# Moving the 2 KB tiles of a two-block network to one run of SBUF addresses

## Chip, core and metric

The kernel runs on one core of one Trainium2 chip. The metric is device time in microseconds, as the median of a few executions. Times inside the kernel come from one execution that the hardware profiler recorded.

## What is computed

The input is 512 tokens of width 1024, in float32. It goes through two blocks of two layers each. In outline:

```python
def first_block(x, ...):          # twice
    p = rmsnorm(x) @ w_in         # latents for attention, and a gated branch
    y_attn = attention(...)       # 8 heads, low-rank q and kv, rotary part
    u = silu(layernorm(dwconv31(a * sigmoid(gt))))
    x = x + concat(y_attn, u) @ w_o
    z = dwconv3(rmsnorm(x) @ w_up)        # 2 * 2816 columns
    x = x + (silu(zg) * zv) @ w_down
def second_block(x, ...):         # layer 0: ssd mixer, layer 1: hgrn2 mixer
    h = layer_norm(ALPHA * x + mixer(x))
    h = layer_norm(ALPHA * h + relu(h @ w1)**2 @ w2)    # 4096 columns
    x = h + sigmoid(h @ w_gate) * (p @ w_proj)
```

All weights are float32 and are read from HBM once, 232.5 MB in all.

## The kernel before

Activations lie transposed: channels on the 128 partitions, the 512 tokens along the free axis. One such tile of float32 takes 2048 bytes in each partition. Nearly everything that is computed with lives in tiles of this size, class `s`; 86 places for them exist (`SLOTS`, line 617). Smaller classes are `r` (3 places of 4096 bytes, where raw weights land), `u` (4 of 2168 bytes, with margins for convolutions), `t` (512 bytes), `n` (up to 128 bytes), and one tile each for the vectors `V` and the constants `C`.

A product in nearly full precision is made of three single-pass float32r matmuls (`mm3`, line 717; `dense`, line 722). An activation and a weight are each split into a rounded part "hi" and the rest "lo" (`pair`, `split_from`, lines 636 and 727; `weights`, line 689), and the three matmuls are hi by hi, lo by hi and hi by lo. Each streams 512 columns (256 where a stage works on half of the tokens, `HALVES`, line 623) past 128x128 weights. The moving operand is a whole `s` tile or a half of it, and the weights are a 512-byte slice of an `s` tile. So both operands of these matmuls start at the address of an `s` tile plus a multiple of 512 bytes. The weights of matmul k+1 are loaded while matmul k streams.

The order of all work is laid down beforehand. Operations are first recorded, then a planner (`schedule`, line 464) gives each one an engine, a place in the order and, for each new tile, a place of its class that is free by then. `issue` (line 589) then writes the instructions out; all of them pass through line 599, which is why the profile shows that line everywhere and the reader has to go by tile names. The planner knows nothing of addresses.

Addresses are given while the instructions are written: `alloc` in `build` asks the pool for the tile the first time that a place is used, and the pool hands out the next free bytes, rounded up to 32. So before the change the classes are mixed in the order of first use. The first byte of the pool is 16512 in each partition. The places of class `s` come to lie as follows:

| places | first byte | last start | start modulo 512 | start modulo 256 |
|---|---|---|---|---|
| s0 to s22 | 30656 | 80320 | 448 | 192 |
| s23 to s44 | 84544 | 136256 | 64 | 64 |
| s45, s46 | 138336 | 140384 | 96 | 96 |
| s47 to s52 | 142464 | 152704 | 128 | 128 |
| s53 | 154816 | 154816 | 192 | 192 |
| s54 to s85 | 156992 | 220480 | 320 | 64 |

Among them lie `V`, `C`, `r`, `u`, some of `t` and `n`; the rest of `t` and `n` end at byte 226784. The `r` tiles start at 448 or 64 modulo 512.

Of the kernel before, what the change touches and what calls it, by code (L numbers as in the profile page):

```python
# [9 lines left out]
F32 = mybir.dt.float32  # L10
# [7 lines left out]
P = 128  # L18
S = 512
# [222 lines left out]
class Ap:  # L242
# [55 lines left out]
    def build(self):  # L298
        x = self.tl.real
        for s in self.steps:  # L300
            if s[0] == "i":
                x = x[s[1]]
            elif s[0] == "r":
                x = x.rearrange(s[1], **s[2])
            elif s[0] == "u":
                x = x.unsqueeze(s[1])
            else:
                x = x.to_broadcast(s[1])
        return x
# [307 lines left out]
SLOTS = {"psum": 8, "r": 3, "s": 86, "u": 4, "t": 12, "n": 24, "V": 1, "C": 1}  # L617
KEEP = {"psum": 2, "s": 18, "u": 2, "t": 6, "n": 16}
SIDE_TAPS = 14
EARLY = 3  # L620
FILL = {"mlp0": [(0, 0)], "mlp1": [(1, 0)]}
FULL = (slice(0, S),)
# [3 lines left out]
def record(R, xT, pos, wts, vecs, consts, pT, outT, dbg=None, stop=None):  # L626
    def tl(shape=(P, S), dt=F32, cls=None):
        b = int(np.prod(shape[1:])) * 4
        cls = cls or ("n" if b <= 128 else "t" if b <= 512 else "s")
        assert cls != "s" or b <= 2048  # L630
        return R.tile(cls, shape, dt)

    def bank():
        return R.tile("psum", (P, S), F32)
# [9 lines left out]
    def vec(name, i=0):  # L644
        o, k = vlay[name]
        return V[:, o + i:o + i + 1]
# [42 lines left out]
    def weights(name, l=None):  # L689

        i = used[0]
        u = units[i]
        assert u[0] == name and (l is None or u[1] == l), (u, name, l)
        used[0] += 1
        c, nk = unit_cols(u), u[3]
        if i not in ahead:
            prefetch(i)
        raw = ahead.pop(i)
        rows, per = [], S // c
        for k in range(0, nk, per):  # L700
            m = min(per, nk - k)
            hi, lo = tl((P, m * c), F32R), tl((P, m * c), F32R)
            src = raw[:, k * c:(k + m) * c]
            copy(hi, src)
            R.either.tensor_sub(lo, src, hi)
            rows += [(hi[:, i * c:(i + 1) * c], lo[:, i * c:(i + 1) * c]) for i in range(m)]
        return rows
# [197 lines left out]
    def mixer1(l):  # L905
# [94 lines left out]
        def conv_tile(j):  # L1000
            R.label, R.bias = f"conv{l}", 100
            acc = bank()
            for k in range(CONV_K - SIDE_TAPS):
                wc = vec(f"w_dw_conv{l}", j * CONV_K + k)
# [4 lines left out]
            side = None  # L1009
            for k in range(CONV_K - SIDE_TAPS, CONV_K):  # L1010
                t = tl()
# [141 lines left out]
    def ssd(op):  # L1153
# [69 lines left out]
        def inputs(g):  # L1223
# [3 lines left out]
            if g == 0:  # L1227
                ws, ps = [weights("ssd_w_in_2") for _ in range(EARLY)], [bank() for _ in range(EARLY)]
                for sl in HALVES:
# [425 lines left out]
def build(tc, xT, pos, wts, vecs, consts, pT, outT, dbg=None, stop=None):  # L1655
    R = Recorder()
    record(R, xT, pos, wts, vecs, consts, pT, outT, dbg, stop)
    R.schedule(SLOTS, KEEP)
    with tc.manual_schedule(), tc.tile_pool(name="sbuf", bufs=1) as sb, \
            tc.tile_pool(name="psum", bufs=1, space=bass.MemoryType.PSUM) as ps:  # L1660
        
        def alloc(t):
            pool = ps if t.cls == "psum" else sb
            name = f"{t.cls}{t.slot}"
            return pool.tile(list(t.shape), t.dt, tag=name, name=name, bufs=1)
        R.issue(tc.nc, alloc)
    return R

# [28 lines left out]
```

## Time and profile before

| | us |
|---|---|
| median of 3 executions | 2714.94 |
| lowest, highest | 2714.61, 2717.44 |
| the profiled execution | 2715.32 |
| its span, first to last instruction | 2713.5 |

The profile shows the busy time of each engine (PE is the matmul engine, PEld its weight loads, DVE, ACT and POOL the vector, scalar and GpSimd engines), the clock that PE was granted, chains of waits, and groups of like instructions. A matmul's own duration in it runs from its first column to the end of its last one and overlaps that of the next matmul by some 160 ns. What one matmul costs in a dense sequence is therefore the step from one start to the next: for a merged row of n matmuls it is (length of the row - duration of one) / (n - 1).

### The profile page before, as it was taken

How to read it: one execution, taken by the hardware profiler on the slowest of the kernel's cores; microseconds unless marked ns; L12 is line 12 of the kernel's file. 1: busy time of each engine (PE TensorE's matmuls, PEld its weight loads, DVE VectorE, ACT ScalarE, POOL GpSimd, SP SyncE). 2: the span in 40 equal slices, each digit the busy share in tenths (PEclk: the TensorE clock that was granted, in tenths of full speed). 3: DMA queues.
4: the chain of work that ended last, by engine and by line, in shares of the span. 5: the costliest groups of instructions: out<-in, count | busy, mean ns of one | idle time of the engine just before them, and what ended most of it. 6: DMA issues, size and time to landing. Idle time of an engine off the chain costs nothing.

```text
span 2713.5 us, 38992 instructions
## 1 busy us (share of the span) xinstructions
PE 2671.4 (98%) x15094; PEld 2212.1 (82%) x15094; DVE 1898.9 (70%) x3222; ACT 1200.9 (44%) x2206; POOL 834.2 (31%) x691
## 2 busy tenths in 40 slices
PE   9999999999999999999999999999999999999999
PEld 7777888888778888888778888888988789888889
DVE  8997676678976666685887675555688787554546
ACT  5874333346764323343664432222367674322223
POOL 3561011235721111232441432232412233223332
PEclk8999999999999999999999999999999999999999
DMA  4123132230131223321113412232231123322320
GB/s 164 35 71 116 63 112 98 101 109 29 59 112 62 86 93 109 110 80 63 51 36 109 148 55 103 87 106 97 73 105 48 64 74 107 107 100 89 109 94 32
DMA packets 69449, 235.00 MB, mean 87 GB/s; under 512 B 7824, under 2 KB 11152, under 8 KB 69264
## 3 DMA queue, kind: packets, MB, share of 16 engines
q1 hardware_dynamic: 69264, 232.51, 25.3%
q8 instruction: 119, 1.95, 0.3%
q14 instruction: 66, 0.54, 0.1%
HBM read 230.38 MB, written 2.10 MB: 86 GB/s over the span
## 4 chain that ended last, share of the span: by engine, by line
PE 91%; DVE 6%; issue 1%; ACT 1%; POOL 0%; DMA 0%; SPq 0%; POOLq 0%; ACTq 0%; DVEq 0%
PE psum L599 91%; DVE s L599 5%; DVE psum L599 1%; ACT s L599 1%; DVE n L599 0%; POOL s L599 0%; DMA s<-xT 0%; DVE u L599 0%; SPq L599 0%; POOLq L599 0%; ACTq L599 0%; DVEq L599 0%
## 5 line engine op out<-in xcount | busy, mean ns | idle before, releaser
L599 PE MATMUL psum<-s,s 128*128 128x512 f32 (+4 forms) x12992 | 2608.2, 365 | 23.9 <-DVE s L599 14.7
L599 PEld LDWEIGHTS psum<-s,s 128*128 128x128 f32 (+2 forms) x12992 | 2116.1, 185 | 459.7 <-issue 23.2
L599 POOL TENSOR_TENSOR s<-r,s 128x512 fp32r<-128x512 f32 (+1 forms) x363 | 502.8, 1400 | 1092.5 <-ACT s L599 819.7
L599 ACT CAST s<-r 128x512 fp32r<-128x512 f32 (+1 forms) x743 | 420.6, 612 | 386.4 <-DMA r<-wts 375.4
L599 DVE TENSOR_TENSOR s<-s,s 128x512 f32<-128x512 f32 (+5 forms) x605 | 415.1, 707 | 68.4 <-ACT s L599 57.6
L599 POOL TENSOR_TENSOR s<-s,s 128x512 f32<-128x512 f32 (+5 forms) x234 | 273.0, 1179 | 539.9 <-ACT s L599 290.4
L599 DVE TENSOR_TENSOR s<-s,psum 128x512 f32<-128x512 f32 (+2 forms) x400 | 225.3, 591 | 266.9 <-PE psum L599 265.3
L599 DVE TENSOR_TENSOR s<-r,s 128x512 fp32r<-128x512 f32 x506 | 401.6, 820 | 5.3 <-ACT s L599 2.7
L599 ACT ACTIVATE s<-s 128x512 f32<-128x512 f32 (+1 forms) x335 | 186.2, 578 | 243.7 <-DVE s L599 240.2
L599 ACT ACTIVATE s<-u,V 128x512 f32<-128x512 f32 x200 | 143.0, 761 | 270.4 <-DVE u L599 270.0
L599 ACT ACTIVATE s<-psum 128x512 f32<-128x512 f32 (+2 forms) x176 | 91.9, 524 | 344.5 <-PE psum L599 342.6
L599 DVE SCALAR_TENSOR_TENSOR s<-u,V,s 128x512 f32<-128x512 f32 x176 | 145.9, 830 | 49.0 <-ACT s L599 47.2
L599 DVE SCALAR_TENSOR_TENSOR s<-psum,s 128x512 f32<-128x512 f32 (+1 forms) x88 | 55.7, 640 | 105.0 <-ACT s L599 104.7
L599 DVE TENSOR_TENSOR u<-psum,s 128x512 f32<-128x512 f32 x88 | 60.7, 690 | 92.3 <-PE psum L599 90.3
L599 ACT COPY s<-psum 128x512 f32<-128x512 f32 (+5 forms) x162 | 76.0, 503 | 79.2 <-PE psum L599 77.8
L599 ACT CAST s<-s 128x512 fp32r<-128x512 f32 (+2 forms) x123 | 72.0, 591 | 74.7 <-DVE s L599 67.5
L599 ACT ACT_TABLE_LOAD x72 | 92.4, 1283 | 8.7 <-DVE s L599 6.8
L599 DVE SCALAR_TENSOR_TENSOR psum<-u,V,psum 128x512 f32<-128x512 f32 x128 | 91.8, 743 | 0.3
L599 PE MATMUL psum<-C,s 128*128 128x128 f32 (+1 forms) x532 | 84.9, 272 | 4.5 <-ACT s L599 3.0
L599 DVE SCALAR_TENSOR_TENSOR s<-psum,V,s 128x511 f32<-128x511 f32 (+4 forms) x90 | 65.5, 743 | 29.8 <-ACT s L599 20.7
L599 PEld LDWEIGHTS psum<-C,s 128*128 128x128 f32 x532 | 67.3, 150 | 20.0 <-ACT s L599 7.2
L599 DVE CAST s<-r 128x512 fp32r<-128x512 f32 (+1 forms) x126 | 56.0, 455 | 39.0 <-DMA r<-wts 38.1
(87 smaller groups left out, 834.7 us busy)
## 6 DMA issues: line engine op xcount, KB each, us to landing
r<-wts SPq DMA_DIRECT2D x415, 512.0 KB, 3.5
r<-wts SPq DMA_DIRECT2D x12, 256.0 KB, 2.6
r<-wts SPq DMA_DIRECT2D x8, 384.0 KB, 3.0
s<-xT SPq DMA_DIRECT2D x8, 256.0 KB, 6.1
s<-pT SPq DMA_DIRECT2D x8, 256.0 KB, 3.0
outT<-s SPq DMA_DIRECT2D x16, 128.0 KB, 1.8
r<-wts SPq DMA_DIRECT2D x9, 128.0 KB, 2.0
V<-vecs SPq DMA_DIRECT2D x1, 479.0 KB, 6.7
```

The costliest lines, as they stand in the source:

```text
L599: getattr(eng, meth)(*[res(a) for a in args], **{k: res(v) for k, v in kw.items()})
```

## The change

Before any other tile is asked for, the pool is asked for a filler that brings its next free byte to a multiple of 512, and then for all 86 places of class `s` in order. With 16512 bytes taken the filler is 384 bytes, so s0 starts at byte 16896 = 33 x 512 and s85 ends at byte 193024. All other classes follow above that, in their order of first use, and end 384 bytes higher than before. Instructions, their order, engines and waits are as before; only addresses differ.

```diff
 SIDE_TAPS = 14
+FIRST = 16512
 EARLY = 3
...
             return pool.tile(list(t.shape), t.dt, tag=name, name=name, bufs=1)
+
+        pad = (0 - FIRST) % 512
+        if pad:
+            sb.tile([P, pad // 4], F32, tag="pad", name="pad", bufs=1)
+        for n in range(SLOTS["s"]):
+            sb.tile([P, S], F32, tag=f"s{n}", name=f"s{n}", bufs=1)
         R.issue(tc.nc, alloc)
```

## Rows read from the trace of the kernel before

**Rows 1.** The page: each engine's busy us and share, and PE's clock in 40 slices.
```profile
PE 2671.4 (98%) x15094; PEld 2212.1 (82%) x15094; DVE 1898.9 (70%) x3222; ACT 1200.9 (44%) x2206; POOL 834.2 (31%) x691
...
PEclk8999999999999999999999999999999999999999
```
**Rows 2.** The page: the chain that ended last, by engine.
```profile
PE 91%; DVE 6%; issue 1%; ACT 1%; POOL 0%; DMA 0%; SPq 0%; POOLq 0%; ACTq 0%; DVEq 0%
```
**Rows 3.** Waits of PE: waiter, releaser, us in total, times, longest.
```profile
PE psum L599 <- DVE s L599: 17.3, 26, 2.2
PE psum L599 <- issue: 10.6, 5, 4.0
PE psum L599 <- ACT s L599: 7.5, 13, 1.5
PE psum L599 <- DVE t L599: 1.1, 1, 1.1
PE psum L599 <- POOL s L599: 0.7, 2, 0.4
```
**Rows 4.** Windows, four long stretches: length, PE, PEld, DVE, ACT, POOL, clock, DMA, GB/s.
```profile
213.70:684.70 471.00, 471.00 (x2049) 383.04 (x2050) 339.16 (x491) 195.38 (x324) 117.26 (x96) 1.00 0.25 87
763.50:1180.60 417.10, 417.10 (x1872) 339.32 (x1873) 287.02 (x439) 155.48 (x261) 70.34 (x51) 1.00 0.31 99
1610.70:1937.20 326.50, 326.50 (x1483) 268.30 (x1484) 170.47 (x229) 84.35 (x152) 95.35 (x71) 1.00 0.28 99
2311.30:2644.20 332.90, 332.90 (x1529) 274.38 (x1530) 171.44 (x229) 87.71 (x162) 107.22 (x78) 1.00 0.29 100
```
**Rows 5.** Groups of PE by form: count | busy us, mean ns of one | idle before.
```profile
L599 PE MATMUL psum<-s,s 128*128 128x512 f32 x9200 | 2256.7, 398 | 10.4 <-DVE s L599 6.2 <-ACT s L599 2.4 <-issue 1.6
L599 PE MATMUL psum<-s,s 128*128 128x256 f32 x2640 | 377.0, 283 | 6.1 <-DVE s L599 4.9 <-ACT s L599 1.1
```
**Rows 6.** Timeline of PE from 213.7 us, two long merged rows: start, length, what, count.
```profile
247.74 363.77 PE L599 MATMUL psum<-s,s 128*128 128x512 f32 x1571
...
615.84 60.98 PE L599 MATMUL psum<-s,s 128*128 128x512 f32 x263
```
**Rows 7.** Groups of PE by form within 300 to 600 us.
```profile
L599 PE MATMUL psum<-s,s 128*128 128x512 f32 x1298 | 300.5, 393 | 0.0
```
**Rows 8.** Timeline of PE, 54.45 to 60.60 us and 1000 to 1006.4 us.
```profile
54.19 6.74 PE L599 MATMUL psum<-s,s 128*128 128x512 f32 x29
...
999.82 6.88 PE L599 MATMUL psum<-s,s 128*128 128x512 f32 x29
```
**Rows 9.** Groups of PE by form in these same two windows.
```profile
L599 PE MATMUL psum<-s,s 128*128 128x512 f32 x29 | 6.7, 389 | 0.0
...
L599 PE MATMUL psum<-s,s 128*128 128x512 f32 x29 | 6.9, 394 | 0.0
```
**Rows 10.** Timeline of PE, 2312.70 to 2313.95 us (matmuls of 256 columns).
```profile
2312.45 1.72 PE L599 MATMUL psum<-s,s 128*128 128x256 f32 x13
```
**Rows 11.** The page: groups of the other engines that read or write these tiles.
```profile
L599 POOL TENSOR_TENSOR s<-r,s 128x512 fp32r<-128x512 f32 (+1 forms) x363 | 502.8, 1400 | 1092.5 <-ACT s L599 819.7
L599 ACT CAST s<-r 128x512 fp32r<-128x512 f32 (+1 forms) x743 | 420.6, 612 | 386.4 <-DMA r<-wts 375.4
...
L599 DVE TENSOR_TENSOR s<-r,s 128x512 fp32r<-128x512 f32 x506 | 401.6, 820 | 5.3 <-ACT s L599 2.7
```
**Rows 12.** The page: DMA issues, raw weights: KB each, us to landing.
```profile
r<-wts SPq DMA_DIRECT2D x415, 512.0 KB, 3.5
```

## What the change should do to the time

> **What bounds the kernel now.** I read the busy times first: PE is busy for 98% of the span, at full clock in all slices but the first [rows 1]. Then the chain of waits: 91% of it is PE itself and 6% DVE [rows 2]. Then PE's own waits: some 37 us in all [rows 3]. Four stretches, 1547.5 us together or 57% of the span, have PE busy without a break while DVE is busy for 51 to 72% and the DMA for 25 to 31% [rows 4]. The reader is to see that over most of the span nothing but the step from one matmul to the next sets the time. The change removes no instruction and no wait, so the question is whether that step, or the duration of another engine's operation, depends on addresses.
>
> **Does the step depend on addresses?** The longest unbroken row holds 1571 matmuls of 512 columns in 363.77 us [rows 6]; with 393 ns for one [rows 7] the step is (363.77 - 0.39) / 1570 = 231.5 ns. Now two rows of the same form, the same count and the same granted clock: 29 matmuls take 6.74 us at 54.19 us and 6.88 us at 999.82 us [rows 8]. With 389 and 394 ns for one [rows 9] the steps are 226.8 and 231.6 ns. What differs is where the operands lie. The trace leaves buffer numbers out, so I laid the 15,094 matmul records beside the program's matmuls in order (a plain float32 one makes two records), which gives each record its addresses by the table of places. In the first row the moving tile, the weights in use and the weights being loaded all start at 64 modulo 256. In the second they are mixed.
>
> Over the whole trace 8,653 steps go from one 512-column float32r matmul to another without a wait (under 260 ns); they belong to the 9,200 of that form [rows 5]. Their mean is 231.24 ns and nearly all lie between 224 and 241. Busy or idle, DVE, ACT and POOL do not move that mean by 0.3 ns. Addresses do. Where the three operands agree modulo 256 the mean is 230.46 (3,253 steps), elsewhere 231.71 (5,400). More telling is the order of steps. [...] By place in an agreeing sequence, the means are 230.95, 231.06, 229.86, 229.13, 229.50, 228.70, 228.26, 228.11, 227.65 and, from the tenth step on, 226.64 (89 steps). Of 235 steps that had three such steps before them and whose operands (the previous moving tile too) agreed, 234 stayed at 226 or 227; of 103 whose operands didn't agree, 8 did. So agreement holds PE in a settled step, and one disagreeing tile throws it out. Before, the starts of tiles have four different remainders modulo 256, so long agreeing sequences are rare.
>
> **The change part by part.**
>
> Matmuls of 512 columns. After the change each `s` tile starts at 0 modulo 512 and each weight slice at a multiple of 512, so all these operands agree all the time. Taking each of the 465 unbroken sequences of before and giving its steps the means by place above, the 2000.9 us become 1965.3: -35.6 us. All steps settled at once would give 8,653 x 4.57 ns = -39.5 us. Only the steps in the four long stretches settled (6,383 of them) would give -29.2 us.
>
> Matmuls of 256 columns. Their 2,537 steps have a mean of 118.1 ns, and agreement doesn't help: agreeing sequences settle at 120. The row of 13 at 2312.45 us shows it: (1.72 - 0.283) / 12 = 119.8 ns [rows 5, 10]. By place this costs +3.3 us, and +4.7 with all settled.
>
> Last matmuls of a sequence. 239 of 512 columns are followed by a plain float32 one. At 4 ns each that is -1 us; the bounds are 0 and -1.1.
>
> Other matmuls. Those with 128 columns or less, and those that read `C`, `t` or `n` tiles, keep the steps they have; I take 0, as their steps of 109 ns show no scatter to win.
>
> Other engines. The DVE subtraction that splits weights takes 684 ns in the median with all three tiles at 64 modulo 128, and 683 with its output at 0; the ACT cast 617 and 618; the POOL subtraction 1299 and 1307; these are among the groups of [rows 11]. I take 0. With bounds of 1 ns either way on their several thousand operations, under work that PE hides, it stays 0.
>
> Raw weights. The `r` tiles move from 448 and 64 to 320 and 448 modulo 512, so their DMAs start no better aligned. They land in 3.5 us [rows 12] and none is among PE's releasers [rows 3]: 0.
>
> What of the gain reaches the end. PE's pieces are 91% of 2713.5 us, or 2,477 us of the chain, while PE is busy for 2,671 [rows 1, 2]; 7% of PE's work lies beside a chain of DVE or ACT, as in attention. I leave 7% of the gain there, 2 us. In the long stretches PE would ask 2% more of DVE, whose share rises from 72 to 74% at most [rows 4], so no new bound appears.
>
> Sum: -35.6 + 3.3 - 1.0 + 2.3 = -31 us on 2715.32 of the profiled execution, which is 0.4 us over the median. From the median, 2714.9 - 31 = 2684 us, 1.1% less. With the bounds the sum runs from -29.2 + 4.7 = -24.5 to -39.5 + 3.3 - 1.1 = -37.3: 2678 to 2690.
>
> **Where the address itself is new.** No `s` tile starts at 0 modulo 256 now, and few matmuls have all three operands at 128. That only agreement counts, and not the common remainder, is borne out for shifts of 128 and 256: sequences at 64 and 320 modulo 512 settle alike, and wherever the last three matmuls and steps were the same but for a shift of 128, the next step was the same too (9 of 9 such histories). For a shift of 64 I have only a handful of steps, mostly alike. This is the main doubt.
>
> The rows show equal matmuls stepping by 226.8 or 231.6 ns according to their operands [rows 8, 9]. [...]
>
> **Rivals.**
> 1. No effect: the scatter belongs to something that goes along with addresses in this program. Price 0, 2714.9 us. Against it, 234 of 235 and 8 of 103.
> 2. A mean gain without settling, because at 0 modulo 512 the rules of succession differ and steps only reach the mean of agreeing ones: 8,653 x (231.24 - 230.46) = -6.7 us, 2708 us. For it, that 0 is untried; against it, the invariance above.
> 3. Slower: at 0 modulo 512 the sequences settle too, but in a step above the present mean, as the 256-column ones do now (120 against 118.1). A step of 236, which is frequent today, costs 8,653 x 4.8 = +41 us: 2756. The point of decision is a settled step of 231.2 ns, in the long stretches above all.
> 4. A better settled step, 224, the lowest seen: 8,653 x 7.2 = -63 us, 2652 us.
>
> That the tiles don't land where the diff says is small: 16512 is the pool's first byte in the program of before too, and the filler's size follows from it.
>
> **How the numbers follow.** Settling at 226.67 gets 0.74, rival 1 0.05, rival 2 0.08, rival 3 0.09, rival 4 0.04. The predicted time is 2684. Its own range, widened for sequences that settle more slowly or a share of the gain that waits take, is 2672 to 2694. With rival 2 the range reaches to 2709, which holds 0.82. About 0.2%, or 5.4 us, is what a measurement of this kernel can tell from no change. Rival 2 lies at its edge, so I give 0.05 of it to faster and 0.03 to the same: faster 0.74 + 0.04 + 0.05 = 0.83, same 0.05 + 0.03 = 0.08, slower 0.09.
>
> **What would show it.** The long row of 1571 matmuls should shrink from 363.77 to 1570 x 0.22667 + 0.39 = 356.3 us, and the mean duration of a 512-column matmul from 393 to 389 ns in the long stretches; rows of 256 columns should step by 120 ns. Counts, PE's releasers and DVE's durations should stay. If the row of 1571 keeps 363 us, rival 1 is right; at 362, rival 2; above 364, rival 3; at 352, rival 4. If the row shrinks as forecast and the time doesn't, the gain went into waits, and PE's waits should have grown by as much.

## The result, and the profile after

The changed kernel takes 2686.57 us (median of 4 runs, 2684.52 to 2688.37), the kernel before 2715.99 us beside it (2714.61 to 2717.44). The ratio is 0.9891, with a 95% interval of 0.9874 to 0.9909. Forecast were 2684 us and faster. The profiled execution took 2684.52 us, 30.8 less than the one of before; the sum had said 31.

The page after: busy time of each engine, PE's granted clock, and the chain that ended last. They answer [rows 1, 2].

```profile
PE 2638.8 (98%) x15094; PEld 2211.2 (82%) x15094; DVE 1900.5 (71%) x3222; ACT 1199.0 (45%) x2206; POOL 836.4 (31%) x691
...
PEclk8999999999999999999999999999999999999999
...
PE 89%; DVE 8%; ACT 1%; issue 1%; POOL 0%; DMA 0%; SPq 0%; POOLq 0%; ACTq 0%; DVEq 0%
```

All counts stay. PE's busy time falls by 32.6 us (2671.4 to 2638.8), while no other engine's moves by more than 2.2 us. PEclk reads as before, but its 9 says only 90% or more; more on that below. The chain has 2 points less of PE and 2 more of DVE: where PE got quicker beside a chain of DVE, it now waits for it.

PE's waits after (waiter, releaser, us in total, times, longest), beside [rows 3]:

```profile
PE psum L599 <- DVE s L599: 18.7, 27, 2.2
PE psum L599 <- issue: 10.2, 5, 3.7
PE psum L599 <- ACT s L599: 8.0, 12, 1.5
PE psum L599 <- DVE t L599: 1.1, 1, 1.1
PE psum L599 <- POOL s L599: 0.7, 2, 0.4
```

They grow by 1.5 us, from 37.2 to 38.7: this view shows little of the gain turned into waits.

The four long stretches of [rows 4], between the same instructions to within one or two matmuls (columns: length, then busy us and count of PE, PEld, DVE, ACT and POOL, granted clock, DMA share, GB/s):

```profile
213.90:676.20 462.30, 462.13 (x2048) 382.49 (x2049) 337.55 (x490) 195.26 (x324) 117.92 (x96) 1.00 0.26 89
755.80:1165.70 409.90, 409.90 (x1872) 339.15 (x1873) 286.41 (x439) 155.36 (x261) 70.13 (x51) 1.00 0.31 101
1591.50:1912.30 320.80, 320.80 (x1482) 268.40 (x1483) 170.69 (x229) 84.23 (x152) 96.03 (x71) 1.00 0.29 101
2285.50:2612.70 327.20, 327.20 (x1530) 274.41 (x1530) 171.61 (x229) 87.76 (x162) 107.59 (x78) 1.00 0.29 102
```

Together they last 1520.2 us where they lasted 1547.5. So 27.3 of the 30.8 us come from stretches in which PE is busy with next to no break (0.17 us in the first): the same work in less time, with PE as the only bound.

The rest, some 3.5 us, is no gain of placement. Windows show short stretches in which PE was granted half its clock (0.50); a step of 512 columns takes 427 ns there. Two of them, 13.6 us near the start and 3.4 us near 214 us, are in both traces. Besides these the trace before has the first four below, the trace after only the last two (length, busy us and count of PE, granted clock, DMA share, GB/s):

```profile
90.60:94.00 3.40, 3.40 (x9) 0.50 0.00 0
1380.80:1384.20 3.40, 3.40 (x17) 0.50 0.03 5
2036.20:2039.60 3.40, 3.40 (x13) 0.50 0.44 154
2118.10:2124.90 6.80, 6.31 (x49) 0.50 0.02 5
...
2092.10:2095.50 3.40, 3.40 (x43) 0.50 0.02 6
2194.50:2197.90 3.40, 3.40 (x14) 0.50 0.00 0
```

Each begins within 2 us of the end of a wait of PE of 0.5 to 4.0 us. With every step of one trace laid beside the same step of the other, those that touch a stretch at half clock in either trace account for -4.0 us, and all others for -26.8. Executions of one kernel differ in this: over the four of the changed kernel the mean granted clock runs from 0.993 to 0.996 and the time from 2688.37 to 2684.52 us, and 13 executions of the kernel before, beside the experiments, were granted 0.993 to 0.997. So the 4.0 us are taken here for the chance of this pair; that the change has no part in them is not shown.

The timeline of PE from 213 us answers [rows 6] (start, length, what, count):

```profile
247.52 356.37 PE L599 MATMUL psum<-s,s 128*128 128x512 f32 x1571
...
608.21 59.89 PE L599 MATMUL psum<-s,s 128*128 128x512 f32 x263
```

And the groups of PE by form, within 300 to 600 us and over the whole span, answer [rows 5, 7] (count | busy us, mean ns of one | idle before):

```profile
L599 PE MATMUL psum<-s,s 128*128 128x512 f32 x1325 | 300.5, 389 | 0.0
...
L599 PE MATMUL psum<-s,s 128*128 128x512 f32 x9200 | 2220.0, 395 | 10.9 <-DVE s L599 6.0 <-ACT s L599 3.0 <-issue 1.6
L599 PE MATMUL psum<-s,s 128*128 128x256 f32 x2640 | 380.4, 284 | 5.8 <-DVE s L599 4.7 <-ACT s L599 1.1
```

The row of 1571 lasts 356.37 us; forecast were 356.3. Its step is (356.37 - 0.39) / 1570 = 226.7 ns, where it was 231.5. In the same 300 us PE now does 1325 matmuls instead of 1298.

### The profile page after: what moved, and what is told of

It is laid out like the page before. It is cut to its first block, busy times and chain, and to the rows that moved or that the text cites. A ratio compares the mean times of both kernels' runs of the same rounds, so it can differ in the third digit from the quotient of the medians.

```text
span 2682.7 us, 38992 instructions
## 1 busy us (share of the span) xinstructions
PE 2638.8 (98%) x15094; PEld 2211.2 (82%) x15094; DVE 1900.5 (71%) x3222; ACT 1199.0 (45%) x2206; POOL 836.4 (31%) x691
## 4 chain that ended last, share of the span: by engine, by line
PE 89%; DVE 8%; ACT 1%; issue 1%; POOL 0%; DMA 0%; SPq 0%; POOLq 0%; ACTq 0%; DVEq 0%
PE psum L599 89%; DVE s L599 6%; DVE psum L599 2%; ACT s L599 1%; DVE n L599 0%; POOL s L599 0%; DMA s<-xT 0%; DVE u L599 0%; SPq L599 0%; ACT L599 0%; POOLq L599 0%; ACTq L599 0%; DVEq L599 0%
## 5 line engine op out<-in xcount | busy, mean ns | idle before, releaser
L599 PE MATMUL psum<-s,s 128*128 128x512 f32 (+4 forms) x12992 | 2574.3, 362 | 23.8 <-DVE s L599 14.2
L599 POOL TENSOR_TENSOR s<-r,s 128x512 fp32r<-128x512 f32 (+1 forms) x363 | 506.5, 1410 | 1067.8 <-ACT s L599 813.1
```

The source lines that it names most:

```text
L599: getattr(eng, meth)(*[res(a) for a in args], **{k: res(v) for k, v in kw.items()})
```

## Experiments

The theory: the step between two 512-column float32r matmuls depends on whether the starts of the moving tile, of the weights in use and of the weights being loaded agree modulo 256, and on nothing else that the change touches. The rivals were that the remainder 0 itself counts, that the low end or the neighbourhood of the places counts, and that a larger multiple alone would do. A second question was how the gain divides: does one disagreeing tile cost only its own steps, or those behind it too? Where a text below gives means over steps, the 15,094 matmul records were laid beside the program's matmuls, as in the prediction.

### Another common remainder: off64

All 2 KB places start at 64 modulo 512 instead of 0.

```diff
-        pad = (0 - FIRST) % 512
+        pad = (64 - FIRST) % 512
```

> All 86 tiles side by side at the low end as in the change, but at 64 modulo 512 instead of 0. If only the agreement of a matmul's operands modulo 256 counts: 2686 us like the change, and the row of 1571 matmuls near 247.5 us takes 356.4 us. If the remainder itself counts (a start on a multiple of 128, 256 or 512 bytes): 2708 to 2716 us and a row of some 363 us.

Measured: 2686.97 us (2685.65 to 2688.08, 4 runs), ratio to the kernel before 0.9898 (0.9884 to 0.9913). The long row in the timeline of PE:

```profile
243.59 356.37 PE L599 MATMUL psum<-s,s 128*128 128x512 f32 x1571
```

It has the same length as at 0. Between 0 and 64 the remainder itself doesn't count, and the main doubt of the prediction is settled.

### The same low end, two remainders: alt128

The places stand side by side at the low end as after the change, but the odd ones are moved 128 bytes against the even ones, so every start is a multiple of 128 and neighbouring names disagree modulo 256.

```diff
-        for n in range(SLOTS["s"]):
-            sb.tile([P, S], F32, tag=f"s{n}", name=f"s{n}", bufs=1)
+        for odd in (0, 1):
+            for n in range(odd, SLOTS["s"], 2):
+                sb.tile([P, S], F32, tag=f"s{n}", name=f"s{n}", bufs=1)
+            if not odd:
+                sb.tile([P, 32], F32, tag="pad2", name="pad2", bufs=1)
```

> All tiles at the low end on multiples of 128 bytes, but even-numbered places at 0 and odd-numbered ones at 128 modulo 512, so that about three of four matmuls have operands that disagree modulo 256. If agreement counts: no settled steps, a mean near 231.5 ns, 2712 to 2720 us, as before the change or a little slower. If it is the start on a multiple of 128, or the low end and the neighbourhood of the tiles: 2686 us.

Measured: 2719.53 us (2714.84 to 2724.82, 10 runs), ratio 1.0015 (1.0005 to 1.0025).

```profile
248.99 363.67 PE L599 MATMUL psum<-s,s 128*128 128x512 f32 x1571
```

The row is as long as before the change (363.77 us in [rows 6]), and the mean step of 512 columns is 231.38 ns. Neither the low end, nor a run of tiles without gaps, nor a multiple of 128 bytes gives anything without agreement.

### The old order, two agreeing remainders: spread

Against the kernel before: places are made in the order of first use, scattered among the other classes as they were, and a filler ahead of a 2 KB place brings it to a multiple of 256. So 26 places start at 0 and 60 at 256 modulo 512.

```diff
...
+            if t.cls != "psum" and name not in seen:
+                seen.add(name)
+                if t.cls == "s" and free[0] % 256:
+                    pad = 256 - free[0] % 256
+                    sb.tile([P, pad // 4], F32, tag=f"pad{name}", name=f"pad{name}", bufs=1)
+                    free[0] += pad
+                free[0] += (most[name] + 31) // 32 * 32
             return pool.tile(list(t.shape), t.dt, tag=name, name=name, bufs=1)
```

> The order of first use of before, with the other classes of tiles in between and s85 near the top of the memory; only a filler ahead of a 2 KB tile brings it to a multiple of 256 where it isn't on one, so tiles lie at 0 or 256 modulo 512. If agreement modulo 256 counts: 2686 us and 356.4 us for the row of 1571. If it is the low end or the tiles lying side by side: 2715 us. If agreement must hold modulo 512: between the two, some 2708 us.

Measured: 2684.82 us (2682.13 to 2686.75, 4 runs), ratio 0.989 (0.9875 to 0.9905).

```profile
243.13 356.37 PE L599 MATMUL psum<-s,s 128*128 128x512 f32 x1571
```

The whole gain is there with the tiles scattered. Agreement modulo 256 is enough, and the kernel needs no common block of places.

### The step by itself: micro

It runs blocks of 72 or 48 float32r matmuls of 512 or 256 columns and, between blocks, 4 or 7 plain float32 matmuls as marks. Each block has its own starts for the four operands. The core of a block, with `h`, `l` as the two weight slices and `mh`, `ml` as the two moving tiles:

```python
                for j, (w, m) in enumerate(((h, mh), (h, ml), (l, mh))):
                    i = 3 * k + j
                    nc.tensor.matmul(b[:, 0:cols], w, m, start=i == 0, stop=i == n // 3 * 3 - 1)
```

> It leaves out the network: only matmuls of float32r on fixed tiles, in blocks of 48 or 72 with a few plain float32 ones between blocks, each block with its own remainders modulo 512 of the four operands (moving hi and lo, weights hi and lo). If agreement modulo 256 alone counts: 226.67 ns per step of 512 columns after at most ten steps in the blocks where all four remainders are 0, 16, 32, 64 or 128 and in the one with the weights 256 further on, and 120 ns for 256 columns; other steps, settled or not, where the weights lie 16 to 224 bytes off the moving tile. If the remainder itself counts, the blocks at 16, 32, 64 and 128 differ from the block at 0. For blocks of mixed remainders no theory gives a number; their steps show whether a placement exists with a step below 226.67 ns (512 columns) or 118 ns (256 columns).

The marks of 4 in PE's timeline, each read in a short window that begins within the mark, so that the row holds its last five records. The rows end blocks of 72 matmuls of 512 columns in this order: all at 0, twice; weights 16, then 32 bytes further than the moving tiles; ...; weights 224, then 256 bytes further; all at 16, at 32, at 64, at 128:

```profile
41.05 0.72 PE L41 MATMUL b<-mark 128*128 128x128 f32 x5
58.28 0.72 PE L41 MATMUL b<-mark 128*128 128x128 f32 x5
75.96 0.72 PE L41 MATMUL b<-mark 128*128 128x128 f32 x5
93.64 0.72 PE L41 MATMUL b<-mark 128*128 128x128 f32 x5
...
199.49 0.72 PE L41 MATMUL b<-mark 128*128 128x128 f32 x5
216.74 0.72 PE L41 MATMUL b<-mark 128*128 128x128 f32 x5
234.20 0.72 PE L41 MATMUL b<-mark 128*128 128x128 f32 x5
251.45 0.72 PE L41 MATMUL b<-mark 128*128 128x128 f32 x5
268.70 0.72 PE L41 MATMUL b<-mark 128*128 128x128 f32 x5
285.94 0.72 PE L41 MATMUL b<-mark 128*128 128x128 f32 x5
```

The differences of starts are the lengths of 72 matmuls with a mark: 17.23 us where all agree, 17.68 with the weights 16 or 32 bytes further, 17.25 with 256 bytes, 17.46 with all four at 16, and 17.24 to 17.25 with all at 32, 64 or 128. The difference of 0.45 us, over 72 matmuls, is 6 ns for each. The mean of the last 24 steps of each block, where the sequence has settled:

| 512 columns | settled step, ns |
|---|---|
| all four agree, at 0, 32, 64 or 128 | 226.67 |
| all four at 16 | 230.0 |
| weights +256 | 226.67 |
| weights +16, +32, +64, +160 or +224 | 233.33 |
| weights +96 / +128 / +192 | 234.42 / 232.67 / 228.88 |

With 256 columns the order is another: 120.0 ns where all agree, and 116.7 to 120 for every other distance of the weights that was tried. The program contains nothing of the network, so the cause lies in the operands' starts. One limit to "only the relation counts" shows here: at 16, the only common start tried that is no multiple of 32, the step is 230.0.

### Every relation in steps of 32 bytes: micro2

The same loop, with all 512 combinations of the starts of `ml`, `wh` and `wl` against `mh` in steps of 32 bytes, and for 256 columns the 64 combinations of the two weights.

> It leaves out the network: blocks of 36 float32r matmuls of 512 columns for all 512 combinations in which the moving lo tile, the weights hi and the weights lo start 0 to 224 bytes (in steps of 32) off the moving hi tile, and blocks of 48 of 256 columns for the 64 combinations of the weights alone. If agreement modulo 256 is the best placement for 512 columns, no combination steps below 226.67 ns; if it is only one of several settled steps, some combination does, and the kernel could gain by it. For 256 columns agreement gives 120 ns, and some combinations of weights near 113 to 116 ns as in the blocks run before.

With 512 columns no combination steps in less than 226.67 ns. All agreeing reaches it, and so does one other (`ml` +160, `wl` +128). The next best take 228.8 to 228.9, the mean of all is 232.1, the worst takes 236.7. So the change has the best step that placement gave anywhere here, and rival 4 (a settled step of 224) shows up in none of these relations.

With 256 columns agreement, at 120 ns, is worse than the mean of all combinations, 118.1. The best have the weights 64 and 192 bytes further, in either order. These are the marks before and behind such a block of 48 in PE's timeline:

```profile
4680.48 0.61 PE L41 MATMUL b<-mark 128*128 128x128 f32 x4
...
4686.40 0.60 PE L41 MATMUL b<-mark 128*128 128x128 f32 x4
```

From mark to mark 5.92 us pass; the settled step is 113.33 ns. Such a placement in the kernel's own stages of 256 columns was not tried on the chip: the places are shared with the stages of 512 columns, which step by 226.67 ns in agreement.

### A few places that disagree: last8 and last2

After the change, the last 8 places (or the last 2) are moved up by 128 bytes.

```diff
         for n in range(SLOTS["s"]):
+            if n == SLOTS["s"] - 8:
+                sb.tile([P, 32], F32, tag="pad2", name="pad2", bufs=1)
             sb.tile([P, S], F32, tag=f"s{n}", name=f"s{n}", bufs=1)
```

> The change, with the last 8 of the 86 places (s78 to s85) moved up by 128 bytes. Of the steps from one 512-column matmul to the next, 27% then have operands that disagree modulo 256. If only those steps lose what they had gained: 27% of some 31 us, 2695 us. If each of them also throws PE out of the settled step, and the next agreeing ones pay the settling by place in the sequence as before the change: a mean of 229.9 ns, some 24 us over the change, 2710 us.

> The same with the last 2 places alone (s84, s85): 8% of the steps disagree. Loss in those steps alone: 8% of 31 us, 2689 us. With settling again after each of them: a mean of 228.2 ns, 9 us over the change, 2695 us.

Measured: last8 2702.33 us (2701.28 to 2707.11, 4 runs), ratio 0.9955 (0.9938 to 0.9971); last2 2693.37 (2690.7 to 2695.5, 4 runs), ratio 0.9915 (0.9901 to 0.993). The long row of each in PE's timeline, last8 first:

```profile
243.58 360.31 PE L599 MATMUL psum<-s,s 128*128 128x512 f32 x1571
```

```profile
247.40 357.25 PE L599 MATMUL psum<-s,s 128*128 128x512 f32 x1571
```

The long row shortens as the number of disagreeing places falls: 363.8 us before the change, 360.3 with 8 such places, 357.3 with 2, 356.4 with none. Laid beside the program, last8 has 2,329 disagreeing steps of 512 columns. Their mean is 232.5 ns, 5.8 above the settled step, or 13.6 us in all; the agreeing steps behind them lose 6.8 us more. In last2 the 693 disagreeing steps (233.1 ns) cost 4.4 us and the steps behind them 0.9 us. Both times lie between their two expectations. So a disagreeing tile costs its own steps more than the forecast's mean of 4.57 ns, and what follows it loses less: 6.8 us over 2,329 is 2.9 ns for each disagreeing step in last8, 0.9 us over 693 is 1.3 ns in last2. Against the same steps of the changed kernel, last8's 512-column steps lose 17.6 us, where the medians are 15.8 apart; last2's lose 4.4, where the medians are 6.8 apart. The profiled executions of last2 and of the changed kernel are 11.0 us apart, and 5.0 of these lie in steps that touch a stretch at half clock. last2 has two such stretches that the changed kernel's trace lacks:

```profile
2013.80:2020.60 6.80, 5.82 (x26) 0.50 0.25 83
2140.10:2143.50 3.40, 3.40 (x62) 0.50 0.02 5
```

What makes up the 2.4 us left between the medians no trace tells: it is half of last2's own scatter of 4.8 us.

## Why the prediction was right, step by step

**That the step depends on addresses.** Right. The trace of before alone had pointed to it, by two rows of one form that differed in their operands [rows 8, 9]. The second of them, a row of disagreeing operands, now reads (timeline of PE from 988.4 us, the same 29 matmuls):

```profile
988.13 6.74 PE L599 MATMUL psum<-s,s 128*128 128x512 f32 x29
```

With 389 ns for one the step is (6.74 - 0.389) / 28 = 226.8 ns, like that of the first. By rival 1, no effect of placement, micro's blocks would be alike; they step by 226.67 and 233.33 ns, so the measurement decides against it. Why the starts matter inside the chip, no run shows.

**512 columns, forecast -35.6 us.** Measured on the same 8,653 steps: -30.8. Of them, 8,636 stayed under 260 ns and give -33.4 us; their mean is 227.4 ns where 227.1 was forecast. The other 17 cost 2.6 us: 11 of them touch a stretch at half clock (1.9 us) and 6 became waits (0.7 us). The forecast took the means by place in a sequence from before, 230.95 to 227.65 over the first nine steps. After the change, in unbroken sequences of the 8,636, they are 233.0, 232.8, 231.4, 229.3, 230.1, 230.0, 228.5, 228.3, 228.6, 227.2, 226.9 and 226.8, then 226.7: the first steps behind a break are slower than forecast. But 7,220 steps lie beyond the twelfth place, and all 8,636 together lie 6.1 us above the settled step of 226.67, 2.1 us more than the forecast's means had put there. The settled step from which the bounds of -39.5 and -29.2 us follow, 231.24 - 4.57 = 226.67 ns, is the one that micro measured where all operands agree.

**One disagreeing tile throws a sequence out.** The direction was right, the size too strong, as last2 and last8 show. What costs a sequence its settled step for some ten places is a break in it: 233.0 ns at the first place behind one, 227.2 at the tenth.

**256 columns, forecast +3.3 us.** Measured +4.1, of which 0.9 lie in ten steps at half clock. Apart from these the mean step rises from 118.13 to 119.39 ns, where 119.42 was forecast. The last long row, in the timeline of PE before:

```profile
2677.05 32.26 PE L599 MATMUL psum<-s,s 128*128 128x256 f32 x271
```

and after:

```profile
2645.76 32.74 PE L599 MATMUL psum<-s,s 128*128 128x256 f32 x271
```

The steps are (32.26 - 0.283) / 270 = 118.4 and (32.74 - 0.284) / 270 = 120.2 ns. Rival 3's mechanism is real, then, but only for this form.

**Last of a sequence, forecast -1 us.** The sign was wrong: +2.6. A step into a plain float32 matmul keeps its length when it holds no wait (231.6 ns before and after, 167 steps), but 4 that held none now hold one, for 1.9 us.

**What is left beside other chains, forecast +2.3 us.** This mechanism shows in attention. Timeline of PE from 50 us, before:

```profile
49.62 37.88 PE L599 MATMUL psum<-s,s 128*128 128x512 f32 x164
88.69 0.38 PE L599 MATMUL psum<-C,s 128*128 128x1 f32 x2 [1.20 <-DVE s L599]
```

and after:

```profile
49.72 37.34 PE L599 MATMUL psum<-s,s 128*128 128x512 f32 x164
89.09 0.38 PE L599 MATMUL psum<-C,s 128*128 128x1 f32 x2 [2.03 <-DVE s L599]
```

PE is through its row 0.54 us sooner and then waits 0.83 us longer for DVE. The term as a whole came out otherwise: all steps outside the three groups above gained 6.7 us. But 6.6 of these lie in steps that touch a stretch at half clock, more of which the trace before has; the others gained 0.1. What other chains kept is better read outside the four long stretches, at full clock: there the steps of 512 columns gained 4.6 us, those of 256 lost 2.7, and steps into a plain float32 matmul, with their waits, lost 2.4. Together with all else that comes to +0.4 us. So waits took about half of what 512 columns won there and the steps of 256 columns the rest: nothing won outside the long stretches reached the end, where the prediction had left 93% of the whole gain to reach it.

So the measured sum is -30.8 + 4.1 + 2.6 - 6.7 = -30.8 us. That it met the forecast's -31 to 0.2 us is luck. At full clock the same terms are -32.7, +3.2, +2.8 and -0.1, together -26.8 us; the missing -4.0 came from stretches at half clock, for which the prediction has no term, since it read the 9 of PEclk as full clock. The mechanism holds, and -26.8 lies within its bounds of -24.5 and -37.3, but the gain of 512 columns was put 2.9 us too high (0.7 of it are new waits), and the last two terms, forecast at +1.3 together, came to +2.7.

**Other engines and the raw weights, forecast 0.** The page after has these groups, beside [rows 11, 12]:

```profile
L599 POOL TENSOR_TENSOR s<-r,s 128x512 fp32r<-128x512 f32 (+1 forms) x363 | 506.5, 1410 | 1067.8 <-ACT s L599 813.1
L599 ACT CAST s<-r 128x512 fp32r<-128x512 f32 (+1 forms) x743 | 420.5, 612 | 388.1 <-DMA r<-wts 376.6
...
L599 DVE TENSOR_TENSOR s<-r,s 128x512 fp32r<-128x512 f32 x506 | 400.4, 818 | 6.8 <-ACT s L599 4.1
...
r<-wts SPq DMA_DIRECT2D x415, 512.0 KB, 3.5
```

The means are 1410, 612 and 818 ns, against 1400, 612 and 820 before, and transfers land in 3.5 us as they did. In these groups the move of the tiles changed no mean by more than 0.7%.

## To carry to other kernels

Where a profile shows PE busy without a break in float32r matmuls of 512 columns, read the step off a long merged row, (length - one) / (count - 1), and compare rows of the same form whose operands lie differently. Start all tiles that such matmuls read at one remainder modulo 256, on a multiple of 32: here it was worth 1.1% with no instruction changed. It didn't matter where in SBUF (the long row took 356.37 us side by side and scattered) or which remainder it was (356.37 us at 0 and at 64, 226.67 ns a step in micro at 0, 32, 64 and 128), and a few stray tiles cost only their own steps and some behind them (13.6 and 6.8 us with 8 places, 4.4 and 0.9 with 2). Don't expect it of streams of 256 columns, which lost 1 to 2 ns a step by it, nor where another engine's chain ends last: outside the long stretches nothing of the gain was left here (the time there rose by 0.4 us at full clock). And before a difference of a few us between two profiles is explained, compare their stretches at half clock.

## What the runs showed of the hardware

- The settled steps are sharp: with 512 columns 226.67 ns in agreement and 233.33 with the weights 16, 32, 64, 160 or 224 bytes further (micro), 236.7 in the worst of 512 relations (micro2).
- The two widths want opposite placements. With 256 columns agreement gives 120.0 ns, weights 64 and 192 bytes further give 113.33, half of the 226.67 of twice the columns.
- A common start of 16 modulo 512, off a multiple of 32, steps by 230.0 ns in micro, 3.3 more than 226.67, though all operands agree.
- One execution has several short stretches at half clock, of 3.4 us and more, in which a step of 512 columns takes 427 ns; between two profiles of this case they made a difference of 4.0 us, and in another pair one of 5.0 us.
